# Seven products instead of eight in four of sixteen groups of an output projection

## The chip, the cores and the metric

The kernel runs on one core of one Trainium2 chip. The metric is the device time of one execution in microseconds (us), the median of several runs. Engines are named as in the profile: PE is TensorE (its weight loads, which overlap the products, are PEld), DVE is VectorE, ACT is ScalarE, POOL is GpSimd, SP is SyncE, which issues the transfers.

## The reference, cut to what matters

One decoder layer on 256 tokens of width 4096: a combined input projection, three groups of heads (windowed attention, mLSTM, cross-attention), each multiplied by its own SiLU gate, then one output projection and a layer norm, all in float32:

```python
mix = jnp.concatenate([a_out, m_out, c_out], axis=-1).astype(x.dtype)   # (1, 256, 4096)
y = jnp.einsum("bse,ed->bsd", mix, w_out)                               # w_out (4096, 4096)
x = layer_norm(DEEPNORM_ALPHA * x.astype(jnp.float32) + y.astype(jnp.float32), ln_g, ln_b)
```

The change lies in the product `mix @ w_out`.

## The kernel before, in words

**Float32 out of three products.** Every operand of a product is kept as two fp32r tiles, hi (the rounded value) and lo (the rest), and a float32 product is hi·hi + hi·lo + lo·hi, three matmuls into one accumulator (`mm3`, L194 to L199; the lo·lo term is left out). Weights are split on the fly by `split` (L91 to L93): ACT casts the raw tile to hi (L92), DVE subtracts hi from raw and so writes lo (L93).

**The output projection** is the end of the kernel. `mix` lies in SBUF as 16 tiles `mixh`, `mixl` with the model axis on the partitions: 32 K-tiles of 128 x 256 tokens. `w_out` is cut into 8 blocks of 512 output columns (b = 0 to 7) and each block into 16 groups (g) of two K-tiles, a group being one raw tile of 128 x 1024 float32 (512 KB). `rows_block` (L206) goes over the groups of a block: for each of two K-tiles and each of two halves of the tokens one `mm3` of 512 columns, so 12 products of 512 columns in a group, accumulated over the block in two PSUM banks. Blocks 0 to 6 go through this loop (L893 to L901). The last block is written out apart (L903 on): token half 1 there has products of 256 columns, and the products of its last 8 groups are held back to the very end.

**What sets the order.** The order of instructions on each engine is the order in which the program is written (`in_order`). `fetch` (L157) issues the load of group g + 2 (`LOOK = 2`): the transfer on SP's queue, the cast on ACT and the subtraction on DVE are written down ahead of the products of group g. The pools `his` and `los` have 3 buffers, so the cast for group g + 2 waits until PE is through with group g - 1; `raws` has 4 buffers of 128 x 1024. `pump` after each group runs what is due of the small work: `after` puts the functions of a finished block one per group behind the next block's groups 0, 1, 2, 3: in the kernel before `residual` (scale and add from PSUM, statistics; L842), `gain` (times ln_g; L847), and the same for the other token half. `later` adds `gain_rows(b - 1)` in block b, four small DVE and four small ACT instructions (L826 to L829).

Accumulators come from two pools of four PSUM banks each, `acc` and `att`. Block 0's accumulators and `last0`, the accumulator of the last block's token half 0, are taken from `acc`; `last1` from `att`.

Of the kernel before, what the change touches and what calls it, by code (L numbers as in the profile page):

```python
# [36 lines left out]
K_ORDER = list(range(16, 24)) + list(range(24, 32)) + list(range(0, 16))  # L37
# [3 lines left out]
def hybrid_layer(ctx, tc, t, out):  # L41
# [3 lines left out]
    nc = tc.nc  # L45
# [3 lines left out]
    unit = ctx.enter_context(tc.tile_pool(name="unit", bufs=34))  # L49
# [10 lines left out]
    def U(name, shape=(P, 4, 256), dt=F32):  # L60
        return unit.tile(list(shape), dt, name=name, tag="u")
# [40 lines left out]
    def load_act(src, dst, c):  # L102
        raw = raw_tile()
        nc.sync.dma_start(raw, src[:, c * 1024:(c + 1) * 1024])
        for u in range(2):
            a = act_tile(u)
            split(a[:, :, 0], a[:, :, 1],
                  raw[:, u * 512:(u + 1) * 512].rearrange("p (a b) -> p a b", a=2))
            dst.append(a)

    def w_tiles(pool):
        if pool == "unit":
            return [U(nm, (P, 1024), F32R) for nm in ("hiu", "lou")]
        return [his.tile([P, 1024], F32R, name="hi", tag="hi"),
                los.tile([P, 1024], F32R, name="lo", tag="lo")]

    def load_w(src, shape, pool=""):
# [4 lines left out]
        split(hi[:, :n], lo[:, :n], raw[:, :n])  # L122
        return [v[:, :n].rearrange("p (a b) -> p a b", a=shape[0]) for v in (hi, lo)]

    def load_first(act, dst, ws):

        ra = raw_tile()
        a = [act_tile(0), act_tile(1)]
        dst.extend(a)

        def act_piece(k):
            r = ra[:, k * 256:(k + 1) * 256]
            nc.sync.dma_start(r, act[:, k * 256:(k + 1) * 256])
            split(a[k // 2][:, k % 2, 0], a[k // 2][:, k % 2, 1], r)

        def w_piece(g, b, k):
            s = slice(k * 512, (k + 1) * 512)
            nc.sync.dma_start(rw[b][:, s], ws[b][g][:, s])
            split(w[b][0][:, s], w[b][1][:, s], rw[b][:, s])

        for g in range(2):
            rw = [raw_tile() for _ in ws]
            w = [w_tiles("") for _ in ws]
            ready.extend([v.rearrange("p (a b) -> p a b", a=2) for v in hl] for hl in w)
            if g == 0:
                for k in range(2):
                    act_piece(k)
                    for b in range(2):
                        w_piece(g, b, k)
            else:  # L150
                for b in range(2):
                    for k in range(2):
                        if b == 0:
                            act_piece(2 + k)
                        w_piece(g, b, k)

    def fetch(look=LOOK):  # L157
# [85 lines left out]
    def plan_rows(b, n=1):  # L243
        stream.extend(("w", wr[bb, g], (2, 512)) for bb in range(b, b + n) for g in range(16))
# [645 lines left out]
    def store(b, i):  # L890
        nc.sync.dma_start(out[i * P:(i + 1) * P, b * 512:(b + 1) * 512], res[b][:, i])

    for b in range(7):  # L893
        load_res(b)
        if b:
            later(partial(gain_rows, b - 1), 4)
        if b == 6:
            later(partial(gain_rows, 6), 4)
            later(partial(gain_rows, 7), 4)
        ps = rows_block(mix_k, 512)  # L900
        after(*[partial(fn, b, ps, i) for i in range(2) for fn in (residual, gain)])  # L901
# [148 lines left out]
```

## Time and profile before

| | |
|---|---|
| median of 3 runs | 1599.09 us (1598.93 to 1601.42) |
| the profiled execution, its own time | 1599.85 us |
| span from its first to its last instruction | 1598.1 us |
| granted TensorE clock, mean of the span | 0.997 of full speed |
| busy: PE, PEld | 1585.4 us (99%), 1356.7 us (85%) |
| busy: DVE, ACT, POOL | 895.6 us (56%), 707.9 us (44%), 1.7 us |
| output projection | from about 1224 us to the end |
| transfers | 311.34 MB, mean 195 GB/s |

Busy time of PE is modelled up to the end of each product, and consecutive products overlap in it; the pace of PE is read from the starts of its products. In the rows further down, a row of the timeline is start, duration, engine, line and what was written from what, with the idle time ahead of it and who ended it in square brackets; a row of the groups is line, engine, operation, tiles and shape, count, then busy us, mean ns of one, and idle us before it.

### The profile page before, as it was taken

To read this page: it belongs to the slowest core of one execution; us is meant where nothing else is said; L and a number is where in the kernel's file an instruction comes from. 1 tells how busy PE (TensorE), PEld (TensorE's weight loads), DVE (VectorE), ACT (ScalarE), POOL (GpSimd) and SP (SyncE) were. 2 spreads that over 40 slices of the span, in tenths; PEclk is the share of its full clock that TensorE was granted. 3 is DMA by queue.
4 is the path that set the end of the run, shared out by engine and by line. 5 is a ranking of instruction groups with operands and counts; after the bars stand their busy time and mean duration, and the time that the engine had idled before them with its cause. 6 is when DMAs were issued, how large, how long until landed. Compare 5 with 4: busy or idle time off the path is not lost.

```text
span 1598.1 us, 21110 instructions
## 1 busy us (share of the span) xinstructions
PE 1585.4 (99%) x8282; PEld 1356.7 (85%) x8282; DVE 895.6 (56%) x1123; ACT 707.9 (44%) x940; POOL 1.7 (0%) x20
## 2 busy tenths in 40 slices
PE   9999999999999999999999999999999999999997
PEld 7788888999888888888888888888888888888886
DVE  5565555545765467544466556555555555555656
ACT  5454444344643444444354435444444344444441
POOL 0000000000000000000000000000000000000000
PEclk9999999999999999999999999999999999999998
DMA  8777654566555555555645554555556765655564
GB/s 261 234 230 229 224 172 153 155 188 201 199 196 171 196 173 179 189 185 199 207 161 176 180 171 165 191 185 188 191 188 236 274 201 199 205 194 194 203 203 146
DMA packets 92081, 311.34 MB, mean 195 GB/s; under 512 B 10517, under 2 KB 13390, under 8 KB 91982
## 3 DMA queue, kind: packets, MB, share of 16 engines
q1 hardware_dynamic: 91982, 310.01, 58.6%
q8 instruction: 64, 1.05, 0.3%
q14 instruction: 35, 0.29, 0.0%
HBM read 305.74 MB, written 4.23 MB: 194 GB/s over the span
## 4 chain that ended last, share of the span: by engine, by line
PE 97%; DMA 2%; DVE 1%; ACT 0%; issue 0%; DVEq 0%; SPq 0%; ACTq 0%
PE cols L229 31%; PE cols L230 16%; PE rows L198 14%; PE rows L199 14%; PE rows L197 14%; DMA raw<-in_w_rows 1%; PE rowsb L198 1%; PE rowsb L197 1%; PE rowsb L199 1%; PE last L198 1%; PE last L199 1%; PE last L197 1%; PE a_s L718 0%; PE a_tp L752 0%; DMA raw<-in_memT 0%; DMA raw<-in_w_cols 0%
## 5 line engine op out<-in xcount | busy, mean ns | idle before, releaser
L93 DVE TENSOR_TENSOR lo<-raw,hi 128x1024 fp32r<-128x1024 f32 (+2 forms) x559 | 662.9, 1187 | 598.1 <-ACT hi L92 597.0
L92 ACT CAST hi<-raw 128x1024 fp32r<-128x1024 f32 (+2 forms) x559 | 569.2, 1019 | 740.5 <-PE rows L199 364.2
L229 PE MATMUL cols<-act,hi 128*128 128x512 f32 x2176 | 763.2, 394 | 0.0
L230 PE MATMUL cols<-act,lo 128*128 128x256 f32 x2176 | 610.5, 281 | 0.3 <-DVE lo L93 0.3
L229 PEld LDWEIGHTS cols<-act,hi 128*128 128x128 f32 x2176 | 409.1, 188 | 93.3 <-issue 0.2
L230 PEld LDWEIGHTS cols<-act,lo 128*128 128x128 f32 x2176 | 409.4, 188 | 1.0 <-DVE lo L93 0.6
L197 PE MATMUL rows<-hi,act 128*128 128x512 f32 (+1 forms) x576 | 215.9, 375 | 0.8 <-ACT hi L92 0.8
L198 PE MATMUL rows<-lo,act 128*128 128x512 f32 (+1 forms) x576 | 213.6, 371 | 0.4 <-DVE lo L93 0.4
L199 PE MATMUL rows<-hi,act 128*128 128x512 f32 (+1 forms) x576 | 213.1, 370 | 0.0
L198 PE MATMUL rows<-lo,mixh 128*128 128x512 f32 x448 | 176.6, 394 | 0.0
L199 PE MATMUL rows<-hi,mixl 128*128 128x512 f32 x448 | 176.6, 394 | 0.0
L197 PE MATMUL rows<-hi,mixh 128*128 128x512 f32 x448 | 176.5, 394 | 0.0
L197 PEld LDWEIGHTS rows<-hi,act 128*128 128x128 f32 x576 | 108.4, 188 | 19.0 <-ACT hi L92 1.5
L198 PEld LDWEIGHTS rows<-lo,act 128*128 128x128 f32 x576 | 108.5, 188 | 17.7 <-DVE lo L93 1.3
L199 PEld LDWEIGHTS rows<-hi,act 128*128 128x128 f32 x576 | 108.4, 188 | 17.0
L198 PEld LDWEIGHTS rows<-lo,mixh 128*128 128x128 f32 x448 | 84.1, 188 | 20.0
L197 PEld LDWEIGHTS rows<-hi,mixh 128*128 128x128 f32 x448 | 84.0, 188 | 19.9
L199 PEld LDWEIGHTS rows<-hi,mixl 128*128 128x128 f32 x448 | 84.1, 188 | 19.8
L92 ACT CAST mixh<-z 128x256 fp32r<-128x256 f32 x24 | 9.8, 407 | 40.2 <-DVE z L790 40.2
L93 DVE TENSOR_TENSOR act<-raw,act 128x512 fp32r<-128x512 f32 (+1 forms) x34 | 21.1, 654 | 9.3 <-ACT act L92 9.3
L197 PE MATMUL rowsb<-hi,act 128*128 128x512 f32 x64 | 25.5, 398 | 0.0
L198 PE MATMUL rowsb<-lo,act 128*128 128x512 f32 x64 | 25.4, 397 | 0.0
(249 smaller groups left out, 752.0 us busy)
## 6 DMA issues: line engine op xcount, KB each, us to landing
raw<-in_w_cols SPq DMA_DIRECT2D x272, 512.0 KB, 3.3
raw<-in_w_rows SPq DMA_DIRECT2D x236, 512.0 KB, 3.3
raw<-in_w_mv SPq DMA_DIRECT2D x48, 344.0 KB, 2.9
raw<-in_xT SPq DMA_DIRECT2D x8, 512.0 KB, 4.1
r<-in_x_res SPq DMA_DIRECT2D x8, 512.0 KB, 4.5
out_y<-r SPq DMA_DIRECT2D x16, 256.0 KB, 2.1
raw<-in_memT SPq DMA_DIRECT2D x7, 512.0 KB, 4.8
raw<-in_w_rows SPq DMA_DIRECT2D x8, 256.0 KB, 4.4
```

The lines of the kernel that those rows point to most:

```text
L92: nc.scalar.copy(hi, raw)
L93: nc.vector.tensor_tensor(lo, raw, hi.bitcast(F32), op=ALU.subtract)
L197: nc.tensor.matmul(o, xh[:, tok], wh, start=first, stop=False)
L198: nc.tensor.matmul(o, xh[:, tok], wl, start=False, stop=False)
L199: nc.tensor.matmul(o, xl[:, tok], wh, start=False, stop=last)
L229: nc.tensor.matmul(ps, wh[:, kk], a, start=(k == 0), stop=False)
L230: nc.tensor.matmul(ps[:, 0], wl[:, kk], a[:, 0], start=False, stop=(k == KT - 1))
```

## The change: what it does

In blocks 1 to 6 the groups 4, 7, 10 and 13 are computed by Strassen's scheme in Winograd's form. Such a group is a 2 x 2 product of blocks: two halves of the tokens by two K-tiles, times two K-tiles by two halves of the 512 columns. It takes seven products of 256 columns, each as three matmuls, instead of eight (the `mm3` of 512 columns counted as two of 256).

- `load_seven`: from the raw weights DVE makes the sums T1 to T4 (three instructions; T4 replaces a quarter of the raw tile in place, T1, T2, T3 go to a second raw tile `sums`). Then raw is split as before into `hi`, `lo`, and the sums into two tiles `hiu`, `lou` of the big pool. For group 4 a quarter of `sums` is zeroed by POOL, and the split covers all 1024 columns; for the others it is two splits of 256 and 512 columns.
- `sums_of`: once, during block 0, DVE makes the sums S1 to S4 of `mix` for the four groups, and ACT and DVE split them.
- `seven_block`: 12 other groups as before; a group of the four issues 21 matmuls of 256 columns, except in group 4, where two of them are 512 wide because they open the accumulators. A block now holds four banks: `seven0`, `seven1` (as before, per token half), `seven2`, `seven3` (the products that several outputs share). Odd blocks take them from `att`, even ones from `acc`.
- `seven_first`, `seven_second` replace `residual` for blocks 1 to 6; the shared products are added there. They stand in the queue behind groups 0 and 1 of the next block, the two `gain` behind groups 2 and 3.

```diff
+SEVEN = (4, 7, 10, 13)
+    def load_seven(src, zero):
+        raw, sums = raw_tile(), raw_tile()
+        nc.sync.dma_start(raw, src)
+        hi, lo = w_tiles("")
+        th, tl = w_tiles("unit")
+        b = raw.rearrange("p (k c n) -> p k c n", k=2, c=2)
+        tv = sums.rearrange("p (a n) -> p a n", a=4)
+        if zero:
+            nc.gpsimd.memset(tv[:, 1], 0.0)
+        nc.vector.tensor_tensor(tv[:, 0:4:3], b[:, :, 1], b[:, 0], op=ALU.subtract)
+        nc.vector.tensor_tensor(tv[:, 2], b[:, 1, 1], tv[:, 0], op=ALU.subtract)
+        nc.vector.tensor_tensor(b[:, 0, 1], b[:, 1, 0], tv[:, 2], op=ALU.subtract)
+        split(hi, lo, raw)
+        for s in ([slice(0, 1024)] if zero else [slice(0, 256), slice(512, 1024)]):
+            split(th[:, s], tl[:, s], sums[:, s])
+        return [hi, lo], [th, tl]
...
+    def sums_of(g):
...
+        nc.vector.tensor_tensor(tmp[:, :512].rearrange("p (k n) -> p k n", k=2), mixh[k // 4][:, s].bitcast(F32),
+                                mixl[k // 4][:, s].bitcast(F32), op=ALU.add)
+        o = tmp[:, 512:].rearrange("p (a n) -> p a n", a=4)
+        nc.vector.tensor_tensor(o[:, 0], v[:, 0, 1], v[:, 1, 1], op=ALU.add)
+        nc.vector.tensor_tensor(o[:, 1], o[:, 0], v[:, 0, 0], op=ALU.subtract)
+        nc.vector.tensor_tensor(o[:, 2], v[:, 0, 0], v[:, 0, 1], op=ALU.subtract)
+        nc.vector.tensor_tensor(o[:, 3], v[:, 1, 0], o[:, 1], op=ALU.subtract)
+        u = U("sums", (P, 2, 4, P), F32R)
+        split(u[:, 0], u[:, 1], o)
...
+    def seven_block(b):
+        ps = [psum(f"seven{n}", (P, 2, 256), att if b % 2 else acc) for n in range(4)]
+        for g in range(16):
+            w = fetch()
+            if g in SEVEN:
...
+                for n, (lhs, vs, at) in enumerate(((a12, w[0], 512), (s4, w[0], 768), (a22, w[0], 256), (s1, w[1], 0),
+                                                   (s3, w[1], 768), (s2, w[1], 512), (a11, w[0], 0))):
...
+                    nc.tensor.matmul(o[:, half_], lhs[0], lo, start=False, stop=False)
+                    nc.tensor.matmul(o[:, half_], lhs[1], hi, start=False, stop=last and n in (4, 6))
...
+    def seven_sum(b, ps):
+        tmp = raw_tile()
+        v = tmp.rearrange("p (a n) -> p a n", a=4)
+        nc.scalar.copy(v[:, 0:2], ps[2])
+        nc.vector.tensor_tensor(v[:, 1], v[:, 0], v[:, 1], op=ALU.add)
+        nc.vector.tensor_tensor(v[:, 2:4], v[:, 1:2].to_broadcast([P, 2, 256]), ps[3], op=ALU.add)
+        return v
+    def seven_first(b, ps):
+        v = seven_sum(b, ps)
...
+        nc.vector.scalar_tensor_tensor(r, r, ALPHA, flat(ps[0]), op0=ALU.mult, op1=ALU.add)
+        nc.vector.tensor_tensor(r[:, :256], r[:, :256], v[:, 0], op=ALU.add)
+        nc.vector.tensor_tensor(r[:, 256:], r[:, 256:], v[:, 2], op=ALU.add)
+        nc.vector.bn_stats(stats[0][:, b], r)
+    def seven_second(b, ps):
...
+        nc.vector.scalar_tensor_tensor(r, r, ALPHA, flat(ps[1]), op0=ALU.mult, op1=ALU.add)
+        rv = r.rearrange("p (a n) -> p a n", a=2)
+        nc.vector.tensor_tensor(rv, rv, v[:, 3:4].to_broadcast([P, 2, 256]), op=ALU.add)
+        nc.vector.tensor_tensor(rv[:, 1], rv[:, 1], ps[3][:, 0], op=ALU.add)
+        nc.vector.bn_stats(stats[1][:, b], r)
+    posts.extend((clock[0] + 4 + 3 * n, partial(sums_of, g)) for n, g in enumerate(SEVEN))
...
-        ps = rows_block(mix_k, 512)
-        after(*[partial(fn, b, ps, i) for i in range(2) for fn in (residual, gain)])
+        if b == 0:
+            ps = rows_block(mix_k, 512)
+            after(*[partial(fn, b, ps, i) for i in range(2) for fn in (residual, gain)])
+        else:
+            ps = seven_block(b)
+            after(partial(seven_first, b, ps), partial(seven_second, b, ps),
+                  *[partial(gain, b, ps, i) for i in range(2)])
```

In the changed file the lines of `split` are L95 and L96, those of `mm3` L221 to L223, `gain` is L876 and `gain_rows` L852 to L855.

**DVE's queue at the start of block 2, before.** These rows stand right behind the subtraction for group 2 (lo is the low half of the weights, r the residual tile, rows the two accumulators of block 1, ln_g the gain); the second lo is that for group 4.

```order
L844 SCALAR_TENSOR_TENSOR r_10890<-r_10890,rows_10892 128x512
L845 BN_STATS stats_10580<-r_10890 128x6
L93 TENSOR_TENSOR lo<-raw,hi 128x1024
L850 TENSOR_TENSOR r_10890<-r_10890,ln_g_10554 128x512
L93 TENSOR_TENSOR lo<-raw,hi 128x1024
L844 SCALAR_TENSOR_TENSOR r_10890<-r_10890,rows_10893 128x512
L845 BN_STATS stats_10581<-r_10890 128x6
```

The same place now, from behind the subtraction for group 2 of block 2 to ahead of the load of group 4 (`seven_10928` to `seven_10931` are the accumulators 0 to 3 of block 1):

```order
L982 TENSOR_TENSOR raw<-raw 128x256
L983 TENSOR_TENSOR raw<-raw,seven_10931 128x512
L990 SCALAR_TENSOR_TENSOR r_10926<-r_10926,seven_10928 128x512
L991 TENSOR_TENSOR r_10926<-r_10926,raw 128x256
L992 TENSOR_TENSOR r_10926<-r_10926,raw 128x256
L993 BN_STATS stats_10580<-r_10926 128x6
L96 TENSOR_TENSOR lo<-raw,hi 128x1024
L998 SCALAR_TENSOR_TENSOR r_10926<-r_10926,seven_10929 128x512
L1000 TENSOR_TENSOR r_10926<-r_10926,raw 128x512
L1001 TENSOR_TENSOR r_10926<-r_10926,seven_10931 128x256
L1002 BN_STATS stats_10581<-r_10926 128x6
```

Ahead of the load of group 4 there stood two subtractions, one pair of residual and statistics and one gain; now there stand two subtractions and ten instructions of `seven_first` and `seven_second`.

**What follows on DVE** is the load of group 4 (three sums, then the two subtractions of its two splits), the gains, groups 5 and 6, and `gain_rows`:

```order
L139 TENSOR_TENSOR raw<-raw 128x2x256
L140 TENSOR_TENSOR raw<-raw 128x256
L141 TENSOR_TENSOR raw<-raw 128x256
L96 TENSOR_TENSOR lo<-raw,hi 128x1024
L96 TENSOR_TENSOR lou<-raw,hiu 128x1024
L876 TENSOR_TENSOR r_10926<-r_10926,ln_g_10554 128x512
L96 TENSOR_TENSOR lo<-raw,hi 128x1024
L876 TENSOR_TENSOR r_10926<-r_10926,ln_g_10554 128x512
L853 TENSOR_TENSOR gb_10563<-ln_g_10554,gb_10563 32x256
L855 TENSOR_TENSOR gb_10563<-ln_b_10555,gb_10563 1x256
```

Two more of these small rows, the subtraction for group 6 and the same load for group 7 come next; before, one subtraction per group stood in place of each load.

**ACT's queue at the last block.** `seven_12878` is the accumulator `seven2` of block 6:

```order
L95 CAST hi<-raw 128x1024 x5
L981 COPY raw<-seven_12878 128x512
L95 CAST hi<-raw 128x1024 x8
L95 CAST hiu<-raw 128x1024 x5
L1081 ACT_TABLE_LOAD
```

The last of the five casts is that for group 2 of the last block; before, there was no copy among these casts. `last0` takes the bank of `seven_12878` (all four banks of `acc` belong to block 6 at that point), so that PE's first product of the last block waits for the copy.

## Rows read from the trace of the kernel before

**Rows 1.** The page: busy time by engine, and the chain's shares by engine.
```profile
PE 1585.4 (99%) x8282; PEld 1356.7 (85%) x8282; DVE 895.6 (56%) x1123; ACT 707.9 (44%) x940; POOL 1.7 (0%) x20
...
PE 97%; DMA 2%; DVE 1%; ACT 0%; issue 0%; DVEq 0%; SPq 0%; ACTq 0%
```
**Rows 2.** Windows, 39 us of the output projection: length, busy by engine, PEclk, DMA, GB/s.
```profile
1387.00:1426.00 39.00, 39.00 (x169) 31.53 (x168) 22.59 (x25) 16.22 (x18) 0.00 (x0) 1.00 0.60 201
```
**Rows 3.** Waits from 1270 to 1550 us: total us, times, longest.
```profile
ACT hi L92 <- PE rows L199: 153.7, 94, 1.8
DVE lo L93 <- ACT hi L92: 116.2, 93, 1.6
```
**Rows 4.** Timeline of ACT: casts of the weights, 15 groups from first to last.
```profile
1279.55 1.05 ACT L92 CAST hi<-raw 128x1024 fp32r<-128x1024 f32 x1 [1.77 <-PE rows L199]
...
1312.92 1.05 ACT L92 CAST hi<-raw 128x1024 fp32r<-128x1024 f32 x1 [1.73 <-PE rows L199]
...
1321.30 1.05 ACT L92 CAST hi<-raw 128x1024 fp32r<-128x1024 f32 x1 [1.73 <-PE rows L199]
1322.25 0.40 ACT L826 CAST gb<-ln_g 64x256 fp32r<-64x256 f32 x1
```
**Rows 5.** Timeline of PE: a block's first product; products of 256 columns, 54 in a row.
```profile
1312.72 0.39 PE L197 MATMUL rows<-hi,mixh 128*128 128x512 f32 x1
...
1570.41 0.28 PE L197 MATMUL last<-hi,mixh 128*128 128x256 f32 x1
...
1576.67 0.28 PE L199 MATMUL last<-hi,mixl 128*128 128x256 f32 x1
```
**Rows 6.** Timeline of DVE at the start of that block.
```profile
1314.00 1.23 DVE L93 TENSOR_TENSOR lo<-raw,hi 128x1024 fp32r<-128x1024 f32 x1 [1.56 <-ACT hi L92]
1315.14 0.68 DVE L844 SCALAR_TENSOR_TENSOR r<-r,rows 128x512 f32<-128x512 f32 x1
1315.86 0.69 DVE L845 BATCH_NORM_STATS2 stats<-r 128x6 f32<-128x512 f32 x1
```
**Rows 7.** Groups by form, DVE and then ACT, whole span.
```profile
L93 DVE TENSOR_TENSOR lo<-raw,hi 128x1024 fp32r<-128x1024 f32 x503 | 615.5, 1225 | 551.3 <-ACT hi L92 550.2
...
L887 DVE SCALAR_TENSOR_TENSOR r<-r,rs_y,ln_ps 128x512 f32<-128x512 f32 x16 | 10.7, 740 | 0.6 <-PE ln_ps L882 0.6
L845 DVE BATCH_NORM_STATS2 stats<-r 128x6 f32<-128x512 f32 x15 | 10.4, 695 | 0.5
L850 DVE TENSOR_TENSOR r<-r,ln_g 128x512 f32<-128x512 f32 x15 | 10.3, 684 | 0.0
...
L236 DVE TENSOR_TENSOR y<-cols,low 128x256 f32<-128x256 f32 x24 | 10.0, 417 | 0.0
L844 DVE SCALAR_TENSOR_TENSOR r<-r,rows 128x512 f32<-128x512 f32 x14 | 9.5, 680 | 0.0
L829 DVE TENSOR_TENSOR gb<-ln_b,gb 1x256 fp32r<-1x256 f32 x16 | 6.7, 422 | 0.5
...
L92 ACT CAST hi<-raw 128x1024 fp32r<-128x1024 f32 x503 | 527.6, 1050 | 684.2 <-PE rows L199 318.0 <-PE cols L229 202.8 <-issue 119.1
...
L760 ACT COPY ao<-a_o 128x512 f32<-128x512 f32 x4 | 2.4, 588 | 9.9 <-PE a_o L350 9.9
```
**Rows 8.** Transfers: count, KB each, median us from issue to landing.
```profile
raw<-in_w_rows SPq DMA_DIRECT2D x236, 512.0 KB, 3.3
...
raw<-in_memT SPq DMA_DIRECT2D x7, 512.0 KB, 4.8
```
**Rows 9.** Windows at the end of the span, columns as in rows 2.
```profile
1584.00:1588.00 4.00, 0.67 (x6) 0.47 (x4) 2.91 (x13) 0.20 (x1) 0.00 (x0) 1.00 0.41 154
1588.00:1590.00 2.00, 1.40 (x5) 0.83 (x5) 0.91 (x3) 0.00 (x0) 0.00 (x0) 0.94 0.00 0
1590.00:1592.00 2.00, 2.00 (x5) 1.01 (x4) 2.00 (x4) 0.00 (x0) 0.00 (x0) 0.50 0.47 175
```
**Rows 10.** Groups by form: memsets of POOL.
```profile
L834 POOL MEMSET col<- 128x97 f32 x2 | 0.4, 181 | 0.0
```

More of the change, by code (lines that the diff above doesn't have):

```diff
@@ L161, in fetch @@
                 load_act(*item[1:])
+            elif item[0] == "seven":
+                ready.append(load_seven(*item[1:]))
             elif item[0] == "first":
@@ L268, in hybrid_layer @@
     plan_cols(28, 40)
-    plan_rows(7, 7)
+    plan_rows(7)
+    stream.extend(("seven", wr[b, g], g == SEVEN[0]) if g in SEVEN else ("w", wr[b, g], (2, 512))
+                  for b in range(8, 14) for g in range(16))
     stream.extend(("w", wr[14, g], (2, 512), "unit" if g >= 11 else "") for g in range(16))
@@ L891, in store @@
         nc.sync.dma_start(out[i * P:(i + 1) * P, b * 512:(b + 1) * 512], res[b][:, i])
+    sums = {}
+    def sums_of(g):
+        k = K_ORDER[2 * g]
+        s = slice(k % 4, k % 4 + 2)
+        tmp = raw_tile()
+        v = tmp[:, :512].rearrange("p (k h n) -> p k h n", k=2, h=2)
+        nc.vector.tensor_tensor(tmp[:, :512].rearrange("p (k n) -> p k n", k=2), mixh[k // 4][:, s].bitcast(F32),
[7 more added lines that the diff above has]
+        split(u[:, 0], u[:, 1], o)
+        sums[g] = [[u[:, n, a] for n in range(2)] for a in range(4)]
@@ new lines, in flat @@
+    def flat(v):
+        return v.rearrange("p a b -> p (a b)")
+    def seven_block(b):
[3 more added lines that the diff above has]
+            if g in SEVEN:
+                (a11, a21), (a12, a22) = [[[v[:, i] for v in mix_k(2 * g + kk)] for i in tiles] for kk in range(2)]
+                s1, s2, s3, s4 = sums[g]
+                (bh, bl), (th, tl) = w
+                last = g == SEVEN[-1]
+                wide = g == SEVEN[0]
+                for n, (lhs, vs, at) in enumerate(((a12, w[0], 512), (s4, w[0], 768), (a22, w[0], 256), (s1, w[1], 0),
+                                                   (s3, w[1], 768), (s2, w[1], 512), (a11, w[0], 0))):
+                    tile_, half_ = ((0, 0), (0, 1), (1, 0), (3, 0), (3, 1), (2, 1), (2, 0))[n]
+                    o = ps[tile_]
+                    hi, lo = [v[:, at:at + 256] for v in vs]
+                    if wide and n == 3:
+                        nc.tensor.matmul(flat(o), lhs[0], vs[0][:, 0:512], start=True, stop=False)
+                    elif wide and n == 5:
+                        nc.tensor.matmul(flat(o), lhs[0], vs[0][:, 256:768], start=True, stop=False)
+                    else:
+                        nc.tensor.matmul(o[:, half_], lhs[0], hi, start=False, stop=False)
+                    nc.tensor.matmul(o[:, half_], lhs[0], lo, start=False, stop=False)
+                    nc.tensor.matmul(o[:, half_], lhs[1], hi, start=False, stop=last and n in (4, 6))
+            else:
+                for kk in range(2):
+                    n = 2 * g + kk
+                    for i in range(2):
+                        mm3(flat(ps[i]), mix_k(n), w, kk, tiles[i], slice(0, 512),
+                            n == 0, n == KT - 1)
+            pump()
+        return ps
@@ new lines, in seven_sum @@
+    def seven_sum(b, ps):
+        tmp = raw_tile()
+        v = tmp.rearrange("p (a n) -> p a n", a=4)
[5 more added lines that the diff above has]
+        v = seven_sum(b, ps)
+        shared[b] = v
+        r = res[b][:, 0]
+        nc.vector.scalar_tensor_tensor(r, r, ALPHA, flat(ps[0]), op0=ALU.mult, op1=ALU.add)
+        nc.vector.tensor_tensor(r[:, :256], r[:, :256], v[:, 0], op=ALU.add)
+        nc.vector.tensor_tensor(r[:, 256:], r[:, 256:], v[:, 2], op=ALU.add)
+        nc.vector.bn_stats(stats[0][:, b], r)
@@ new lines, in seven_second @@
+    def seven_second(b, ps):
+        v = shared[b]
+        r = res[b][:, 1]
+        nc.vector.scalar_tensor_tensor(r, r, ALPHA, flat(ps[1]), op0=ALU.mult, op1=ALU.add)
[3 more added lines that the diff above has]
+        nc.vector.bn_stats(stats[1][:, b], r)
+    shared = {}
+    posts.extend((clock[0] + 4 + 3 * n, partial(sums_of, g)) for n, g in enumerate(SEVEN))
@@ L899, in hybrid_layer @@
             later(partial(gain_rows, 7), 4)
-        ps = rows_block(mix_k, 512)
-        after(*[partial(fn, b, ps, i) for i in range(2) for fn in (residual, gain)])
+        if b == 0:
+            ps = rows_block(mix_k, 512)
+            after(*[partial(fn, b, ps, i) for i in range(2) for fn in (residual, gain)])
+        else:
+            ps = seven_block(b)
+            after(partial(seven_first, b, ps), partial(seven_second, b, ps),
+                  *[partial(gain, b, ps, i) for i in range(2)])
     load_res(7)
```

## The prediction

> **What bounds the kernel now.** I began with the page: PE is busy for 99% of the span and makes 97% of the chain that ended last [rows 1]. The windows then say how much room the others have where the change lies: in 39 us of the output projection PE has no gap, the granted clock is 1.00, DVE works 22.59 us and ACT 16.22 us [rows 2]. The waits there are all ahead of ACT and DVE: ACT waits for PE to free a weight buffer, DVE for ACT's cast [rows 3]. So PE sets the pace, and DVE is idle for 42% of the time. But DVE cannot save up that time: a cast may start only when PE has left the group three earlier, so weights are at most two groups ahead. What counts is therefore not the sum of DVE's work over a block but its deadlines, group by group.
>
> The pace of PE: two casts 15 groups apart start at 1279.55 and 1321.30 [rows 4], so a group takes 2.78 us, a product of 512 columns 0.232. Of 54 products of 256 columns in a row the first and the last start 6.26 us apart [rows 5], 0.118 each, with a weight load ahead of each. The narrow products thus cost no more per column, and the scheme's saving is real on PE.
>
> The deadline pattern, at the start of a block: PE's first product at 1312.72 [rows 5], the cast for group 2 at 1312.92 [rows 4], its subtraction at 1314.00 [rows 6], 1.28 us after the block's start. From there DVE's order is fixed.
>
> **The change, part by part. PE:** an ordinary group of the four has 21 products of 256 columns, 21 x 0.118 = 2.48 us, 0.30 less than 2.78; group 4 has 19 of those and two of 512, 2.71 us, 0.07 less. A block saves 3 x 0.30 + 0.07 = 0.97 us, six blocks 5.8 us. That is all there is to win.
>
> **DVE, durations** [rows 7]: a subtraction of 1024 columns 1.225, 512 columns 0.684 (gain), 0.680 (residual), 0.695 (statistics), 256 columns 0.417; a small row of `gain_rows` 0.422. No row shows the sums with their strides; I take these values by size, since rows of PSUM and SBUF operands agree in them. Upper bound: the dearest row of 512 columns, 0.740, so 0.06 more per sum. **Gaps:** behind the subtraction of 1314.00 the next instruction, which waits for nothing, starts 0.09 before its end; the statistics, which need the residual, 0.04 after the residual's end [rows 6]. I take +0.04 for each instruction that waits (for ACT, a transfer or its forerunner on DVE) and -0.09 for the others.
>
> The Trainium skill (VectorE: DVE Perf Modes, The DRAIN you can't avoid) says that a semaphore after each of a chain of instructions costs nothing extra. These rows show 0.13 us between the two kinds; by the page all gaps would be -0.09 and the time that of the lower bound below.
>
> **The chain of a block 2 to 5,** from its start, in us: 1.28; subtraction of group 2, 1.27; `seven_first` (417, 684, 680, 417, 417, 695 ns, gaps -0.02 together) 3.29; group 3, 1.14; `seven_second` 2.64; group 4: three sums 1.64, wait for ACT's cast 1.09, subtractions 1.27 and 1.14, together 5.13; gain 0.72; group 5, 1.14; gain 0.72; `gain_rows` 4 x 0.46 = 1.84; group 6, 1.27; group 7: sums 1.64, cast 1.09, subtraction 1.23. Sum 24.4 us. PE wants that last result for its second product of group 7: 4 x 2.78 + 2.71 + 2 x 2.78 + 0.12 = 19.5 us. **DVE is 4.9 us late, and PE waits for it**, first at group 4 (chain 13.3 against 11.2 + 0.1, so about 2), the rest at groups 5, 6 and 7. From group 7 on, three groups cost DVE 5.18 + 2 x 1.27 = 7.7 us and PE 2.48 + 2 x 2.78 = 8.0, so nothing more is lost, and the plain groups 14 to 1 clear the queue; each block starts afresh. Four blocks: 19.6 us.
>
> **Block 1** has the plain residuals of block 0 behind it and one of them after group 4, so groups 4 to 7 are in time (chain to group 7: 18.6 against 19.5). `gain_rows` falls between groups 7 and 8: 1.28 + 1.14 + 1.46 + 0.2 (group 3's cast) + 1.14 + 0.72 + 5.13 + 1.46 + 1.14 + 0.72 + 1.27 + 5.18 + 1.84 + 1.23 = 23.9 against 4 x 2.78 + 2.71 + 2 x 2.78 + 2.48 + 0.23 = 22.1: 1.7 us. **Block 6** has 4.9 like the others, and two more sets of `gain_rows`, ahead of groups 10 and 14, of 1.84 us each against 0.3 to 0.5 us regained: 2.8 us; 7.7 together.
>
> **ACT at the last block:** PE's first product waits for the copy of `seven2`, which stands behind the cast for group 2, and that cast waits for PE's last product of block 6. Nothing hides it: 0.20 to the cast [rows 4, 5], 0.95 until the next instruction starts (1321.30 to 1322.25) [rows 4], 0.59 for a copy of 512 columns from PSUM [rows 7]: 1.7 us.
>
> **Hidden:** `sums_of` in block 0, 3.4 us of DVE with its wait for a cast, four times; DVE idles 1.5 us of each group [rows 3], and its subtraction comes 3.3 us before PE's need, so the 1.9 us of delay is absorbed. POOL's memset of 256 columns (97 columns take 0.18 us [rows 10]) ends long before its cast. Bytes are unchanged; but each of the four groups takes two raw buffers, so the transfer for group 10 is asked for only when group 7's subtraction is done, and DVE is back for it 3.7 us later, against a landing of 3.3 [rows 8]: in time, by 0.4.
>
> **Sum:** 19.6 + 1.7 + 7.7 + 1.7 - 5.8 = +24.9 us on the profiled execution's 1599.85 gives 1624.8; that lies 0.76 above the median of the runs, so I say 1624.0. **Bounds:** with all gaps -0.09, 23 waits of a chain fall by 0.13, and a block loses 1.9 us, block 1 none, block 6 2.4: 4 x 1.9 + 2.4 + 1.7 - 5.8 = +5.9, 1605. With the sums 0.06 dearer (12 in a chain, 0.7 us a block) +4, and with landings of 4.8 us [rows 8], which hold up groups 10 and 13 by some 1.3 us a block, +8: 1636.
>
> **Rivals.** *VectorE keeps up:* the mean speaks for it: some 40 us of DVE in a block against PE's 43.6. It would need the chain to group 7 to be 4.9 us shorter, that is under 19.5 us, say because gaps vanish and the small rows run beside others. Then only the copy at the last block is lost: 1599.1 - 5.8 + 1.7 = 1595, faster than before. Against it: the durations are each seen many times, and the chain is serial on one queue. Chance 5%.
>
> *The transfers become late:* with one buffer less ahead, each four-group load asks late; if landings under bunched requests reach 5.5 us, groups 10 and 13 (and 4 of the next block) wait 2.2 us more than 3.3, some 3.4 us a block, 17 to 20 us more: 1642. For it: the margin is 0.4 us; against it: 0.60 of the DMA engines' time is used [rows 2] and the bytes per us fall. Chance 10%.
>
> *The clock falls:* PE's waits of 1 to 2 us come in clusters at groups 4 to 7. In the trace PE worked 0.67 us of 4, and the granted clock was still 1.00, then 0.94 and 0.50 in the next windows [rows 9], the lower of its levels (1.2 GHz). If each block after its waits ran 4 us at the lower level, where a product takes twice the time, six blocks would lose 12 us more: 1636. Against it: around these waits PE stays some 80% busy. Chance 7%. The Trainium skill (TensorE: Matmul & The Clock Gate, HAM oscillation) describes just this loss in loops where PE waits between bursts of products; the trace shows the fall only in the sparse end.
>
> *The scheme saves nothing on PE,* if narrow products with changing weights and accumulators were dearer than 0.118: then the 5.8 us go and the time is 1630. The last block's rows have the same loads. Chance 3%.
>
> **How the numbers follow.** The forecast has 75%, the rivals 25%. The range 1610 to 1636 takes in most of the way to the lower bound, the dearer sums with late landings, the fallen clock and the scheme without saving; outside lie the 5% of a faster kernel, the 10% of late transfers and some of the lowest times. 0.2% (3.2 us) is about what a measurement of this kernel can tell from no change; faster by more: 0.05, the first rival; within it: 0.03, from the tail between that and the lower bound; slower: 0.92.
>
> **What would show it.** In the profile after: PE idle at the second product of groups 4 and 7 of blocks 2 to 6 with the subtraction `lo` as its releaser, some 1 to 2 us each; nearly none in block 1; blocks 2 to 5 taking 48.4 us against 44.5 now; one wait of 1.7 us at the first product of the last block, ended by ACT; DVE busy without gaps from group 2 to group 7. Wrong would make it: DVE gaps near zero or below, PE waiting for transfers, a granted clock under 1.00 in blocks 2 to 6, or products of 256 columns at another pace than 0.118.

## The result, and the profile after

| | before | changed |
|---|---|---|
| median of 4 runs each | 1599.55 us (1598.93 to 1601.42) | 1626.15 us (1625.52 to 1626.38) |
| ratio, 95% interval | | 1.0162 (1.0150 to 1.0174) |
| profiled execution, own time and span | 1599.85, 1598.1 us | 1625.52, 1623.6 us |
| granted clock, mean of the span | 0.997 | 0.992 |

The change makes the kernel 26.6 us slower. The page answers to [rows 1]; first the busy time by engine, then the chain's shares:

```profile
PE 1591.2 (98%) x8498; PEld 1367.5 (84%) x8498; DVE 977.6 (60%) x1297; ACT 730.3 (45%) x992; POOL 3.6 (0%) x26
...
PE 85%; DVE 8%; DMA 3%; ACT 2%; issue 1%; SPq 0%; ACTq 0%; DVEq 0%
```

DVE is busy for only 60% of the span, 82 us more than before, and yet it now makes 8% of the chain that ended last. The waits from 1270 to 1600 us (total us, times, longest) answer to [rows 3]:

```profile
ACT hi L95 <- DVE raw L141: 104.8, 22, 7.6
...
PE seven L966 <- DVE lo L96: 8.4, 11, 0.9
...
PE seven L965 <- ACT hi L95: 4.6, 5, 1.6
```

PE, which had no wait in these blocks before, now waits for the low half of the weights, and for ACT's cast. ACT in turn waits for the third sum (L141): both go back to DVE.

**Where the time lies.** PE's timeline, the first product of block 0, then the first product of group 14 (the first plain group behind the last of the four) of blocks 1 to 6, and the first product of the last block:

```profile
1224.39 0.40 PE L221 MATMUL rows<-hi,mixh 128*128 128x512 f32 x1
...
1309.17 0.40 PE L221 MATMUL seven<-hi,mixh 128*128 128x512 f32 x1
...
1357.14 0.39 PE L221 MATMUL seven<-hi,mixh 128*128 128x512 f32 x1
...
1405.87 0.39 PE L221 MATMUL seven<-hi,mixh 128*128 128x512 f32 x1
...
1455.17 0.39 PE L221 MATMUL seven<-hi,mixh 128*128 128x512 f32 x1
...
1503.14 0.39 PE L221 MATMUL seven<-hi,mixh 128*128 128x512 f32 x1
...
1552.23 0.39 PE L221 MATMUL seven<-hi,mixh 128*128 128x512 f32 x1
...
1560.37 0.50 PE L221 MATMUL last<-hi,mixh 128*128 128x512 f32 x1 [1.62 <-ACT raw L981]
```

The same two ends in the timeline of the kernel before:

```profile
1223.57 0.40 PE L197 MATMUL rows<-hi,mixh 128*128 128x512 f32 x1
...
1535.59 0.39 PE L197 MATMUL last<-hi,mixh 128*128 128x512 f32 x1
```

Before, seven blocks took 312.02 us, 44.57 each. PE's own work in a block with the scheme is 43.60 us (run 9 below shows blocks of 43.61), 0.97 less. What lies above it is loss:

| part | forecast | measured |
|---|---|---|
| PE saves, six blocks | -5.8 | -5.8 |
| block 1 | +1.7 | +2.2 (84.78 us for blocks 0 and 1 up to group 14; 82.6 without waits) |
| blocks 2 to 5 | +19.6 | +19.6 (47.97, 48.73, 49.30 and 47.97, each less 43.60) |
| block 6 | +7.7 | +6.3 (49.09 - 43.60, and 0.8 in its last two groups) |
| the last block's first product | +1.7 | +1.8 |
| sum, block 0's start to the last block's | +24.9 | +24.1 (335.98 - 312.02 = 23.96) |
| ahead of block 0, and after the last block's start | 0 | +0.8, +0.7 |

That is 25.5 us between the spans of the two profiled executions; the medians lie 26.6 us apart, since the changed kernel's profiled execution is 0.6 us below its median and the other 0.3 above.

**The chain on DVE, block 2,** answers to [rows 6]. The block starts at 1309.17 + 24 x 0.232 = 1314.74.

```profile
1316.00 1.23 DVE L96 TENSOR_TENSOR lo<-raw,hi 128x1024 fp32r<-128x1024 f32 x1 [1.55 <-ACT hi L95]
1317.14 0.42 DVE L982 TENSOR_TENSOR raw<-raw 128x256 f32<-128x256 f32 x1
1317.60 0.69 DVE L983 TENSOR_TENSOR raw<-raw,seven 128x512 f32<-128x512 f32 x1
...
1319.71 0.69 DVE L993 BATCH_NORM_STATS2 stats<-r 128x6 f32<-128x512 f32 x1
1320.32 1.21 DVE L96 TENSOR_TENSOR lo<-raw,hi 128x1024 fp32r<-128x1024 f32 x1
...
1323.96 0.67 DVE L139 TENSOR_TENSOR raw<-raw 128x512 f32<-128x512 f32 x1
...
1325.13 0.42 DVE L141 TENSOR_TENSOR raw<-raw 128x256 f32<-128x256 f32 x1
1326.80 1.23 DVE L96 TENSOR_TENSOR lo<-raw,hi 128x1024 fp32r<-128x1024 f32 x1 [1.24 <-ACT hi L95]
...
1337.33 1.23 DVE L96 TENSOR_TENSOR lo<-raw,hi 128x1024 fp32r<-128x1024 f32 x1 [1.25 <-ACT hi L95]
```

From 1316.00 to 1338.56 DVE stands still for more than 0.05 us only for the two casts. The first of these casts starts on ACT 0.17 us behind the third sum, which ends at 1325.13 + 0.42 = 1325.55:

```profile
1325.72 1.05 ACT L95 CAST hi<-raw 128x1024 fp32r<-128x1024 f32 x1 [6.94 <-DVE raw L141]
```

DVE's subtraction for group 7 ends at 1338.56, 23.8 us after the block's start; PE wanted it 19.5 us after it. The 4.3 us between them are the block's loss. PE's waits at groups 4 and 7 of that block, and in block 5 at groups 4, 6 and 7:

```profile
1326.82 0.39 PE L965 MATMUL seven<-hi,mixh 128*128 128x256 f32 x1 [0.73 <-ACT hi L95]
1328.08 0.39 PE L966 MATMUL seven<-lo,mixh 128*128 128x256 f32 x1 [0.88 <-DVE lo L96]
...
1338.61 0.39 PE L966 MATMUL seven<-lo,mixh 128*128 128x256 f32 x1 [0.47 <-DVE lo L96]
...
1472.83 0.38 PE L965 MATMUL seven<-hi,mixh 128*128 128x256 f32 x1 [0.73 <-ACT hi L95]
1474.09 0.39 PE L966 MATMUL seven<-lo,mixh 128*128 128x256 f32 x1 [0.88 <-DVE lo L96]
...
1480.62 0.50 PE L222 MATMUL seven<-lo,mixh 128*128 128x512 f32 x1 [0.60 <-DVE lo L96]
...
1484.61 0.39 PE L966 MATMUL seven<-lo,mixh 128*128 128x256 f32 x1 [0.88 <-DVE lo L96]
```

**The clock fell in blocks 2, 3 and 4.** The windows behind group 4 of block 2, and the same stretch of block 5 (length, busy by engine, granted clock, DMA, GB/s):

```profile
1324.00:1328.00 4.00, 2.47 (x10) 1.50 (x8) 2.69 (x6) 2.28 (x3) 0.00 (x0) 1.00 0.52 150
1328.00:1332.00 4.00, 3.92 (x21) 3.82 (x22) 3.94 (x7) 3.22 (x6) 0.00 (x0) 0.66 0.47 140
...
1472.00:1476.00 4.00, 2.39 (x17) 2.09 (x17) 3.19 (x4) 3.92 (x7) 0.00 (x0) 1.00 0.30 95
1476.00:1480.00 4.00, 4.00 (x21) 3.01 (x19) 3.84 (x7) 1.32 (x2) 0.00 (x0) 1.00 0.55 205
```

In block 2 the products behind the two waits ran at the lower level (1.2 GHz) for some 3 us, in block 5, behind the same two waits, they did not; both blocks take 47.97 us. Whether the fall costs anything there is for the experiments.

**Transfers were late in blocks 3 and 4.** In block 3 DVE's sums for group 10 waited for one, in block 4 ACT's cast for group 2:

```profile
1391.22 0.69 DVE L139 TENSOR_TENSOR raw<-raw 128x512 f32<-128x512 f32 x1 [1.48 <-DMA raw<-in_w_rows]
```

```profile
1412.54 1.05 ACT L95 CAST hi<-raw 128x1024 fp32r<-128x1024 f32 x1 [1.63 <-DMA raw<-in_w_rows]
```

Block 4 starts at 1405.87 + 5.57 = 1411.44, so the chain begins 0.9 us later than in block 2 (cast at 1314.92, 0.18 after the start). Blocks 3 and 4 exceed 47.97 by 0.8 and 1.3 us: in block 3 that is the late transfer, in block 4 the late transfer gives 0.9. The other 0.4 us go with the fallen clock: it stood at the lower level longer than in block 2 (0.54 of full speed in the window below, and 0.61 in the 4 us ahead of it), and PE reached group 7 only 0.45 us after DVE's subtraction for it had ended (1434.93 + 1.23 = 1436.16).

```profile
1428.00:1432.00 4.00, 4.00 (x17) 3.63 (x16) 3.85 (x7) 0.93 (x1) 0.00 (x0) 0.54 0.47 158
```

```profile
1434.93 1.23 DVE L96 TENSOR_TENSOR lo<-raw,hi 128x1024 fp32r<-128x1024 f32 x1 [1.25 <-ACT hi L95]
```

```profile
1436.61 0.28 PE L965 MATMUL seven<-hi,mixh 128*128 128x256 f32 x1
```

### The profile page after: what moved, and what is told of

Same layout as the page of the kernel before. It is cut to its first block, busy times and chain, and to the rows that moved or that the text cites. A ratio compares the mean times of both kernels' runs of the same rounds, so it can differ in the third digit from the quotient of the medians.

```text
span 1623.6 us, 21812 instructions
## 1 busy us (share of the span) xinstructions
PE 1591.2 (98%) x8498; PEld 1367.5 (84%) x8498; DVE 977.6 (60%) x1297; ACT 730.3 (45%) x992; POOL 3.6 (0%) x26
## 4 chain that ended last, share of the span: by engine, by line
PE 85%; DVE 8%; DMA 3%; ACT 2%; issue 1%; SPq 0%; ACTq 0%; DVEq 0%
PE cols L253 30%; PE cols L254 15%; PE rows L222 8%; PE rows L221 8%; PE rows L223 8%; DVE lo L96 3%; DMA raw<-in_w_rows 2%; PE seven L222 2%; PE seven L223 2%; PE seven L221 2%; ACT hi L95 2%; PE rowsb L222 1%; PE rowsb L221 1%; PE rowsb L223 1%; DMA raw<-in_w_cols 1%
## 5 line engine op out<-in xcount | busy, mean ns | idle before, releaser
L96 DVE TENSOR_TENSOR lo<-raw,hi 128x1024 fp32r<-128x1024 f32 (+2 forms) x559 | 661.4, 1187 | 533.4 <-ACT hi L95 532.4
L95 ACT CAST hi<-raw 128x1024 fp32r<-128x1024 f32 (+2 forms) x559 | 568.1, 1019 | 732.1 <-PE cols L253 206.9
L221 PE MATMUL rows<-hi,act 128*128 128x512 f32 (+1 forms) x576 | 215.5, 374 | 1.8 <-ACT hi L95 1.8
L223 PE MATMUL rows<-hi,act 128*128 128x512 f32 (+1 forms) x576 | 212.6, 369 | 0.0
L221 PEld LDWEIGHTS rows<-hi,act 128*128 128x128 f32 x576 | 108.2, 188 | 20.3 <-ACT hi L95 2.9
L223 PEld LDWEIGHTS rows<-hi,act 128*128 128x128 f32 x576 | 108.1, 188 | 17.0
L222 PE MATMUL seven<-lo,mixh 128*128 128x512 f32 x288 | 114.5, 398 | 3.1 <-DVE lo L96 3.1
L221 PE MATMUL seven<-hi,mixh 128*128 128x512 f32 x288 | 114.2, 397 | 0.0
L223 PE MATMUL seven<-hi,mixl 128*128 128x512 f32 x288 | 113.7, 395 | 0.0
L222 PEld LDWEIGHTS seven<-lo,mixh 128*128 128x128 f32 x288 | 54.5, 189 | 16.8 <-DVE lo L96 4.9
L223 PEld LDWEIGHTS seven<-hi,mixl 128*128 128x128 f32 x288 | 54.4, 189 | 12.6
L221 PEld LDWEIGHTS seven<-hi,mixh 128*128 128x128 f32 x288 | 54.6, 190 | 11.8
L96 DVE TENSOR_TENSOR lou<-raw,hiu 128x256 fp32r<-128x256 f32 (+2 forms) x47 | 31.7, 709 | 2.2 <-ACT hiu L95 2.2
L966 PE MATMUL seven<-lo,mixh 128*128 128x256 f32 x72 | 22.2, 308 | 8.4 <-DVE lo L96 8.4
L95 ACT CAST hiu<-raw 128x256 fp32r<-128x256 f32 (+2 forms) x47 | 28.0, 633 | 3.1 <-DMA raw<-in_w_rows 3.1
L95 ACT CAST mixh<-z 128x256 fp32r<-128x256 f32 x24 | 9.8, 407 | 40.3 <-DVE z L816 40.3
```

The lines of the kernel that those rows point to most:

```text
L221: nc.tensor.matmul(o, xh[:, tok], wh, start=first, stop=False)
L222: nc.tensor.matmul(o, xh[:, tok], wl, start=False, stop=False)
L223: nc.tensor.matmul(o, xl[:, tok], wh, start=False, stop=last)
L966: nc.tensor.matmul(o[:, half_], lhs[0], lo, start=False, stop=False)
```

## The experiments

The theory: VectorE cannot work ahead, and its queue from a block's start up to group 7 holds more than PE takes for those groups. Rivals: transfers, because each group of the four takes two raw buffers; the clock; narrow products that save nothing; the mean load of VectorE.

**1. The bank of `last0` alone.**

```diff
-    ps0 = acc.tile([P, 512], F32, name="last0", tag="acc")
+    ps0 = att.tile([P, 512], F32, name="last0", tag="att")
```

> Only the PSUM bank of last0 is changed: it comes from the pool that block 6 does not use, so that PE's first product of the last block no longer waits for the copy of seven2. Theory (the copy is on the path): the wait of 1.6 us ended by ACT at the first product of the last block goes and nothing takes its place, 1626.15 - 1.7 = 1624.5 us. Rival (the weights of the last block's first groups are late as well, so that the wait only changes its releaser): within 0.5 us of 1626.15.

1624.79 us (1623.59 to 1626.99). PE's timeline, first product of group 14 of block 6 and of the last block:

```profile
1552.15 0.39 PE L221 MATMUL seven<-hi,mixh 128*128 128x512 f32 x1
...
1558.55 0.39 PE L221 MATMUL last<-hi,mixh 128*128 128x512 f32 x1
```

6.40 us in place of 1560.37 - 1552.23 = 8.14, and no wait ahead of the last block: the term of 1.7 us is shown in the trace. In the medians (1.4 us) it is smaller than the scatter of the runs.

**2. The four groups two places later.**

```diff
-SEVEN = (4, 7, 10, 13)
+SEVEN = (6, 9, 12, 14)
```

> Only the places of the four groups change, from 4, 7, 10, 13 to 6, 9, 12, 14: the same work on every engine, but the first two loads with sums stand two groups further behind seven_first, seven_second, the gains and gain_rows. Deadline theory (VectorE's chain from the block's start is late at groups 4 and 7): PE gains 4.6 us for the two groups of delay, the chain by then has two subtractions and gain_rows more ahead of its first load; working the chain forward with the durations of the trace gives blocks 2 to 5 of about 45.5 us in place of 48.0 to 49.3, block 1 about 1 us less, and 1615 us (1612 to 1618). Rival, transfers: loads of two raw buffers each are as many and closer together (12, 14), so 1626 or more. Rival, mean load of VectorE: the sum of its work is unchanged, so 1626.

1620.16 us (1619.32 to 1624.19), ratio to the kernel before 1.0130 (1.0116 to 1.0143). Moving the work without changing it gains 6 us, so mean load is out, but the gain is half of what was expected, and the time lies above the expected range. Block 4, from group 14 to group 14, takes 45.6 us, close to the 45.5 worked out; blocks 2 and 3 take 48.3 and 48.5. ACT's timeline and the window behind group 6 of block 2 show why:

```profile
1313.04 1.05 ACT L95 CAST hi<-raw 128x1024 fp32r<-128x1024 f32 x1 [1.48 <-DMA raw<-in_w_rows]
```

```profile
1334.00:1338.00 4.00, 4.00 (x19) 3.52 (x18) 2.47 (x4) 0.00 (x0) 0.00 (x0) 0.77 0.76 244
```

The transfer for group 2 is late again (likely because groups 12 and 14 take two buffers each shortly before), and the clock falls. Both were left out of the expectation.

**3. Without the sums.**

```diff
-        if zero:
-            nc.gpsimd.memset(tv[:, 1], 0.0)
-        nc.vector.tensor_tensor(tv[:, 0:4:3], b[:, :, 1], b[:, 0], op=ALU.subtract)
-        nc.vector.tensor_tensor(tv[:, 2], b[:, 1, 1], tv[:, 0], op=ALU.subtract)
-        nc.vector.tensor_tensor(b[:, 0, 1], b[:, 1, 0], tv[:, 2], op=ALU.subtract)
+        nc.gpsimd.memset(tv, 0.0)
```

> Leaves out part of the computation: the three sums of each load of the four groups are not made, the tile for them is only filled with zeros by POOL; casts, subtractions, the second raw buffer, all products and the work of seven_first and seven_second stay. Deadline theory: the chain up to group 7 loses two times three sums (1.6 us each) and two waits for the cast (1.2 us each), 5.7 us, more than the 4.4 us by which it is late; the waits at groups 4 to 7 go, what stays is the saving of PE, the 1.7 us at the last block and about 1 us of rests: 1599.55 - 5.8 + 1.7 + 1 = 1596.5 us (1595 to 1600), below the kernel before. Rival, transfers (two raw buffers per group): waits stay, over 1615. Rival, the narrow products save nothing on PE: 1602 or more even without waits.

1597.47 us (1596.45 to 1599.51), ratio 0.9985 (0.9976 to 0.9994): below the kernel before. First products of group 14 of blocks 1 and 2:

```profile
1308.18 0.40 PE L217 MATMUL seven<-hi,mixh 128*128 128x512 f32 x1
...
1351.96 0.39 PE L217 MATMUL seven<-hi,mixh 128*128 128x512 f32 x1
```

43.78 us, 4.2 less than 47.97, with the same products, casts, subtractions and two raw buffers per group. So the narrow products save nearly all that was forecast, and the loss hangs on VectorE's sums, together with the pauses for the casts that have to wait for them.

**4. PE kept at work in the waits of group 4.**

```diff
+                warm = mixh[0][:, 0:2].rearrange("p a b -> p (a b)")
+                for x in range(3 if wide else 0):
+                    nc.tensor.matmul(flat(ps[2]), a12[0], warm, start=True, stop=True)
...
+                    for x in range(4 if wide and n == 0 else 0):
+                        nc.tensor.matmul(flat(ps[3]), a12[0], warm, start=True, stop=True)
```

> In blocks 1 to 6 PE gets seven more products of 512 columns at group 4 (three ahead of its first product, four ahead of its second), written into banks that the group then opens anew, so that the result is unchanged: 1.62 us of work in the two waits of group 4 (0.7 to 1.6 and 0.9 us in blocks 2 to 6). Theory (VectorE sets the time there, the fallen clock of blocks 2, 3 and 4 is hidden behind the same waits): granted clock stays nearer to 1.00 in those blocks, and the time stays, 1626 to 1628 us (block 1, which does not wait at group 4, loses up to 1.6 us). Rival (the clock costs of itself what the products at the lower level show, 1.3, 1.4 and 2.3 us in blocks 2, 3 and 4): about 1621 to 1623 us.

1629.07 us (1627.67 to 1631.04), ratio 1.0181 (1.0167 to 1.0195). The granted clock is 1.00 in all windows from 1270 to 1558 us; in block 2:

```profile
1328.00:1332.00 4.00, 4.00 (x27) 3.38 (x26) 3.97 (x6) 3.62 (x7) 0.00 (x0) 1.00 0.42 135
```

Block 2 takes 1309.56 to 1357.51, 47.95 us: as long as with the fall. The rival on the clock falls for this block, and the time does not go to its 1621 to 1623. It is a little above the 1626 to 1628 expected; block 0 and block 1 up to group 14 take 1.1 us more (85.88 in place of 84.78), within what was expected there.

**5. Five raw buffers.**

```diff
-    raws = ctx.enter_context(tc.tile_pool(name="raws", bufs=4))
+    raws = ctx.enter_context(tc.tile_pool(name="raws", bufs=5))
```

(One buffer of a pool of small tiles is given up for it.)

> One raw buffer more (five of 128 x 1024 in place of four; a small pool gives up one of six tiles that it does not need). Theory (VectorE's chain; transfers matter only where they delay its start: the cast for group 2 waited for a transfer in blocks 3 and 4 of the changed kernel, whose lengths are 0.8 and 1.3 us over the others): 1623 to 1625.5 us, and the waits at groups 4 and 7 stay. Rival (two raw buffers per group of the four are the main cause): below 1612 us.

1617.59 us (1617.20 to 1618.72), ratio 1.0111 (1.0095 to 1.0126): more than expected, less than the rival. First products of group 14 of blocks 1 to 5:

```profile
1306.10 0.40 PE L221 MATMUL seven<-hi,mixh 128*128 128x512 f32 x1
...
1354.08 0.39 PE L221 MATMUL seven<-hi,mixh 128*128 128x512 f32 x1
...
1402.03 0.39 PE L221 MATMUL seven<-hi,mixh 128*128 128x512 f32 x1
...
1450.00 0.39 PE L221 MATMUL seven<-hi,mixh 128*128 128x512 f32 x1
...
1497.97 0.39 PE L221 MATMUL seven<-hi,mixh 128*128 128x512 f32 x1
```

Four blocks of 47.98, 47.95, 47.97 and 47.97 us. The lengths 48.73 and 49.30 are gone, so those 2.1 us came with the late transfers (in block 4 with the clock's longer fall as well, behind a longer wait); the waits at groups 4 to 7 stay. The clock fell here in blocks 4 to 6 and not in 2 and 3, and blocks 4 and 5 are no longer than 2 and 3. Of the other 4.8 us of span, 2.1 lie ahead of block 0 (it starts at 1222.33), 1.0 in block 1, 0.2 in block 6 and 1.5 behind the last block's start (61.7 us in place of 63.2).

**6. `gain_rows` late.**

```diff
-            later(partial(gain_rows, b - 1), 4)
+            posts.append((clock[0] + 14, partial(gain_rows, b - 1)))
```

> gain_rows of blocks 0 to 5 moves from behind group 5 to behind group 13 of the block in which it runs; the two extra sets of block 6 stay. Deadline theory: its four rows, 1.84 us, leave the chain ahead of group 7, 1.9 us less in each of blocks 2 to 6 and about 0.9 in block 1: the waits of group 4 stay, that of group 7 shrinks or goes, 1617 us; but where the clock falls behind group 4 and VectorE is no longer late at group 7, the slower products cost something of their own (they did in the run with the groups moved later), so 1616 to 1622. Rival, mean load of VectorE: same work, 1626. Rival, transfers: 1626.

1619.24 us (1615.53 to 1620.81), ratio 1.0118 (1.0105 to 1.0132). Taking four small rows out of the chain gains 6.9 us. The wait of group 7 in block 2 is gone, but that block takes 47.26 us (1306.87 to 1354.13) where 1.9 us less than 47.97 was expected: VectorE is now in time at group 7, and the fallen clock shows.

**7. The same with PE kept at work,** the edit of run 4 for blocks 2 to 6 on top of run 6.

> The run with gain_rows late, and in blocks 2 to 6 the seven extra products of 512 columns at group 4, as in the run that kept PE busy there. In that run the extra work gained nothing, since VectorE was late again at group 7 whatever the clock did. Here VectorE is in time at group 7. Theory: the fall of the clock then costs what the slow products show (some 1.2 us in block 2, 2.3 in block 5, more at the end of block 6); with the clock held at 1.00 the time is 1614.5 to 1617 us against 1619.24. Rival (the fall never costs anything): 1619 or more.

1617.66 us (1615.44 to 1618.12), ratio 1.0104 (1.0090 to 1.0117). The medians (1.6 us apart, ranges overlapping) do not settle it. In the traces block 2, group 14 to group 14, takes 46.06 us (1307.58 to 1353.64) at a granted clock of 1.00 against 47.26 with the fall. So the fall cost about 1.2 us in this block, where nothing else is late; that PE's waits bring it about is likely from runs 4 and 7, where work in them left no 4 us window from 1270 to 1558 us below 1.00.

**8. VectorE's work spread by its deadlines, four raw buffers.** The groups are 6, 9, 12, 14; gains and the small rows of `gain_rows` run while VectorE waits for ACT's cast of a changed raw tile; the rows for the last two blocks move to block 1; `last0` as in run 1.

```diff
-        split(hi, lo, raw)
+        nc.scalar.copy(hi, raw)
+        if fillers:
+            fillers.popleft()()
+        nc.vector.tensor_tensor(lo, raw, hi.bitcast(F32), op=ALU.subtract)
...
+            posts.append((clock[0] + 3, partial(gain_rows, b - 1, True)))
+        if b == 1:
+            posts.append((clock[0] + 7, partial(gain_rows, 6, True)))
+            posts.append((clock[0] + 5, partial(gain_rows, 7)))
...
+            gains = [partial(gain, b, ps, i) for i in range(2)]
+            if b < 6:
+                fillers.extend(gains)
```

> The same seven products, with VectorE's work spread by its deadlines: the four groups are 6, 9, 12, 14; the gains and the small rows of gain_rows run inside the loads of the four groups, in the 1.2 us in which VectorE waits for ACT's cast of the changed raw tile; the rows of the last two blocks are made in block 1 in place of block 6; last0 has the other bank. Deadline theory: working the order forward with the durations of the trace leaves no wait of PE in blocks 1 to 6, 43.6 us each, and none at the last block: 1599.55 - 5.8 = 1593.7, with rests of 0.2 us a block 1595 us; late transfers with four raw buffers can add up to some 5 us: 1594 to 1599. Rival, mean load of VectorE or dearer narrow products: no better than 1599.6.

1596.44 us (1594.92 to 1598.88), ratio 0.9982 (0.9973 to 0.9991): faster than the kernel before, with blocks of 43.6 to 44.8 us.

**9. The same with five raw buffers.**

> The same as the run before it, with five raw buffers. Deadline theory: no wait for transfers either, 1593.5 to 1595.5 us, about 0.3% under the kernel before. Rival (transfers never mattered): the same time as with four. Rival (mean load of VectorE or dearer narrow products): no better than 1599.6.

1592.51 us (1590.87 to 1592.78), ratio 0.9953 (0.9940 to 0.9965). The page's first line, a stretch of DVE's timeline and PE's timeline (first product of block 0, of group 15 of blocks 1 and 2, of the last block):

```profile
PE 1579.6 (99%) x8498; PEld 1364.0 (86%) x8498; DVE 975.4 (61%) x1297; ACT 730.4 (46%) x992; POOL 3.6 (0%) x26
```

```profile
1367.60 0.68 DVE L887 TENSOR_TENSOR r<-r,ln_g 128x512 f32<-128x512 f32 x1
1368.93 1.23 DVE L146 TENSOR_TENSOR lo<-raw,hi 128x1024 fp32r<-128x1024 f32 x1 [0.65 <-ACT hi L143]
```

```profile
1222.68 0.40 PE L225 MATMUL rows<-hi,mixh 128*128 128x512 f32 x1
...
1308.19 0.39 PE L225 MATMUL seven<-hi,mixh 128*128 128x512 f32 x1
...
1351.80 0.39 PE L225 MATMUL seven<-hi,mixh 128*128 128x512 f32 x1
...
1529.01 0.39 PE L225 MATMUL last<-hi,mixh 128*128 128x512 f32 x1
```

VectorE does the same work as in the changed kernel, 975.4 us against 977.6, and the kernel is 33.6 us faster (29.7 already with four raw buffers, run 8). The time is 1 us below the expected range. A block takes 43.61 us. The gain (L887) stands in the pause between the third sum and the subtraction, which shrinks from 1.24 to 0.65 us.

**10. The kernel before with five raw buffers.**

> The kernel before with five raw buffers and no other edit, to tell what of the gain of the last version is the buffer's and what the scheme's. If the scheme gives what PE's products say (6 x 0.97 us), this kernel takes 1592.5 + 5.8 = 1598.3 us, 1 to 1.5 us under the kernel before (the changed kernel with five buffers reached the projection 2 us earlier and had a tail 1.5 us shorter). Rival (the buffer alone gave the gain): 1593 us.

1597.92 us (1596.38 to 1598.45), ratio 0.9980 (0.9971 to 0.9989), so the buffer by itself gives 0.2%. From block 0's start to the last block's it takes 1534.40 - 1222.38 = 312.02 us, as before; run 9 takes 306.33. The scheme itself gives those 5.7 us.

## Why the prediction was right, and which of its terms were off

- **What bounds the kernel.** That VectorE's deadlines decide and not its sum was right: runs 2 and 6 only move its work, run 8 moves it and changes one bank, run 9's busy time is that of the changed kernel, and the times lie between 1626 and 1592 us.
- **PE's saving, 0.97 us a block:** 44.57 - 43.61 = 0.96 (run 9).
- **The chain of blocks 2 to 5.** 4.9 us a block were forecast; the chain alone gives 4.4 (47.97 - 43.60, run 5). Two of its prices were off, in opposite directions. A cast behind the third sum was taken at 1.09 us and a gap of 0.04; DVE's pause there is 1.24, since ACT starts 0.17 us after the sum's end (1325.55 to 1325.72). And +0.04 us was charged to every instruction that waits, but most of those whose wait had long been met start 0.08 to 0.09 before their forerunner's end: the subtraction at 1320.32 behind the statistics that end at 1320.40, the sums at 1323.96 likewise. Six such places in the chain take off 0.8 us, the two casts add 0.2. A wait for the forerunner on DVE itself leaves +0.04 (1317.14 + 0.42 to 1317.60). So do the small rows of `gain_rows` and the subtraction behind them (1332.88 + 0.42 to 1333.33), which need nothing of their forerunner; why, no run shows. The Trainium skill (VectorE: DVE Perf Modes, The DRAIN you can't avoid) says that the semaphore adds nothing; this trace agrees where the wait was long met (but for those small rows) and not where the forerunner is waited for.
- **The sum of these blocks was right partly by luck.** Of their 19.6 us, 17.5 are the chain, 1.7 late transfers and 0.4 the fallen clock in block 4; both stood in a rival and not in the sum. The transfers' mechanism was right in kind (the transfer for group 10 in block 3, group 2's in block 4). Their price of 17 to 20 us was at least five times too high: with a fifth buffer (run 5) blocks 1 to 6 are 3.3 us shorter in all.
- **Where PE waits.** The prediction had the second product of groups 4 and 7; ACT's cast is late as well, so the first product of group 4 waits too (0.73 us). The single waits are shorter than the 1 to 2 us forecast: in block 5 four of 0.60 to 0.88 us share the loss. The working's 13.3 us for the chain up to group 4 is not the sum of its terms, which is 13.6; the total does not use it.
- **Block 1** lost 2.2 us for 1.7: PE waits behind group 7 as forecast (1.14 us), and 0.23 us at group 5, which was not. The 18.6 us that the working has for the chain to group 7 there is not the sum of its terms either, which is 19.6 against the 19.5 wanted. **Block 6** lost 6.3 for 7.7: each of the two further sets of `gain_rows` was taken to cost 1.4, they cost 1.9 together over the chain's 4.4. Between two loads more was regained than the 0.3 to 0.5 us of the working, likely because its gaps were too long.
- **The last block's first product:** 1.7 forecast, 1.8 measured; run 1 takes it away alone.
- **The clock.** The rival's fall did happen, in three blocks; a granted clock under 1.00 stood among the forecast's own signs of being wrong. Its price of 12 us was wrong for this kernel: while VectorE is late at group 7, a slower PE only waits less there (runs 4 and 5). Where VectorE is not late, it costs: 0.4 us in block 4, 1.2 in a block of run 6 (against run 7). The Trainium skill (TensorE: Matmul & The Clock Gate, HAM oscillation) describes the fall and its loss for a loop in which PE waits for transfers between bursts of products; the trace here shows the fall without the loss in block 2.
- **What was called hidden.** `sums_of` cost nothing, as forecast: block 1's first product starts at 1268.97, 44.58 us after block 0's, against 44.57 a block before. DVE's idle time per group was read as 1.5 us; [rows 3] give 116.2 / 93 = 1.25.
- **The remaining 1.5 us** (0.8 ahead of block 0, 0.7 behind the last block's start) were in no term. Block 0 started between 1223.4 and 1225.6 us in the profiled executions with four raw buffers here, so the first is within their scatter. The second lies behind the projection's last product, which starts 14.5 us ahead of the end in place of 13.7; its cause is open.

## What to carry to other kernels

When a saving on the bounding engine is paid for by another engine that is half idle, write down that engine's queue from each point at which it cannot have worked ahead, and compare it with the time at which each result is wanted: here 60% busy was too much, and the same work in another order was not. A pause in which an engine waits for its own result to come back from another is the place for work that nobody waits for. The loss of one late chain can hide another (here that of a fallen clock), which appears only when the chain is shortened.

## What the runs showed that was not expected

- **The clock fell behind the same waits in some blocks and not in others:** with 0.73 and 0.88 us of wait at group 4 it fell in blocks 2 and 3 and stayed at 1.00 in block 5, and in run 5 the other way round. In the 4 us from 1324 and from 1472 shown above, PE was busy for 2.47 us ahead of a fall and for 2.39 where none came. What decides it is open.
- **A fifth raw buffer speeds up the kernel before** by 0.2% although PE waits for nothing in its seven blocks: they keep their 312.02 us, and the gain lies ahead of them (1222.38 against 1223.57) and behind.
